# Retention stage of a hybrid diffusion step: query scaling tied to an earlier step, squares summed by ScalarE, weight halves and sums of quarters re-placed

## The chip, the core and the metric

One kernel, one core of one Trainium2 chip. The metric is the time of one execution on the device, in microseconds (us); the kernel before has a median of 1134.67 us over three runs (1134.26 to 1134.86).

## What is computed

One layer of a diffusion backbone on 640 tokens (128 of context, 512 latent; in the kernel five tiles of 128), model width 1024. Two mixers read the same normalised input: grouped-query attention and a bidirectional retention in chunks of 128 tokens. Their outputs are projected, gated, merged and projected again, and a gated MLP with a convolution follows. The change lies in the retention branch and just behind it. The reference, cut to that:

```python
def retention_scan(q, k, v, log_gamma, s0):       # chunks n of 128 tokens
    scores = einsum("bhnid,bhnjd->bhnij", qc, kc) * intra_decay
    intra  = einsum("bhnij,bhnjv->bhniv", scores, vc)
    kv     = einsum("bhnjd,bhnjv->nbhdv", kc * k_decay, vc)
    s_final, s_prev = scan(lambda s, kv_n: chunk_decay * s + kv_n, s0, kv)
    cross  = einsum("bhnid,nbhdv->bhniv", qc * q_decay, s_prev)
    return intra + cross, s_final

def retention_branch(...):                         # both directions, 8 heads, dk 64, dv 128
    o = rms_scale(o_f + o_b)                       # o * rsqrt(mean(o*o) + eps), per token and head
    return silu(rg) * o, s_f, s_b
# then: y = sigmoid(ga) * (ya @ w_att_o) + sigmoid(gr) * (yr @ w_ret_o);  y @ w_out
```

## The kernel before

**Precision.** TensorE multiplies numbers that are split in a high and a low half (`mm3`: three products for one). A weight tile is split by `w_split`: ScalarE casts the high half (L147), and VectorE subtracts it for the low half (L152). With `lo_eng` set to "dma", ScalarE instead writes the negated weights and GpSimd's queue issues a DMA that adds on top of them (L149, L150). The tiles that hold weights before the split are called raw (two in turn), the halves wh (eight in turn).

**Stages.** Normalisation and modulation; keys, values and queries; attention; the attention's output projection; the projections for the retention; the chunk states; the retention itself; a long stage of matrix products by units ("seven"), which computes the second half of the gate, the merge gates and the retention's output projection with seven products in place of eight; then the output projection and the MLP. TensorE accumulates in PSUM banks of 512 numbers per partition: five banks named mm for `mm3` and three named aux, taken in turn.

**Chunk states** (`states`, L968 to L1002). For each of two halves hh of the heads (four heads each) and each tile t: VectorE scales the keys by their decay (L977, twice, into a tile named r2k, five in turn), TensorE multiplies them with the values (L980), ScalarE copies the result out (L985, L990, L992). Then VectorE runs the recurrence in small steps (L997 and L999, 24 each per half). Sums and differences of quarters of the input, needed later by the units (`h_sums`, L928 to L965), are interleaved, and so is the first gate projection `rg0`, an `a_group` over five banks, with two halves of 512 weight rows, twelve matmuls per tile and half (L159 to L161).

**Retention** (`retention`, ten groups (t, hh), t from 0 to 4 within each hh). Four steps per group, each step of a group standing beside other steps of its neighbours:

- `ret_q` (L1009 to L1017): four small transfers on SyncE's queue bring the queries of the group into a tile qd (four in turn, L1015). No transfer for t = 0.
- `ret_a`: TensorE transposes the keys (L1023), ScalarE copies queries and keys (L1027, L1031), VectorE multiplies qd by its decay (L1029).
- `ret_b`, one step later: score products on TensorE into an aux bank (L1040), VectorE multiplies them by the decay matrix into an r2k tile (L1042), which empties the bank.
- `ret_c`, one step later: TensorE multiplies scores with values and qd with the state into an aux bank (L1049, L1051); ScalarE squares the bank into an r2k tile (L1054) and copies it over the values (L1055); VectorE reduces the squares to four sums (L1056, into sso).
- `ret_d`, after each five groups: the root of the sums of squares, twenty numbers per partition (on VectorE by three Newton steps, L210 to L222, for hh = 0; through a power on GpSimd for hh = 1), then the scaling of the outputs, one tile at each step.

`rg0` goes on in between; `evac_rg` (L1113 to L1116) applies the gate to the outputs as its banks finish.

**What sets the order.** Through these stages a scheduler places the instructions of TensorE, VectorE and ScalarE by its own estimate of when each can go; the code's order is only its input. `tc.issue_after(x)` makes what is issued inside it come after x. From L1342 on the engines keep the order in which the code is written (`manual_schedule`): `ret_unit` and `in_unit` prepare weight halves (ScalarE's cast L1173, VectorE's subtraction L1193), and a list `plan` of pairs (n, step) says behind which product n of the sequence each further step is issued. Through `plan` go the transposed outputs (`yr_block`, L1365 and L1370), and the halves of their quarters and sums of quarters: L1414 subtracts two quarters into yx, `y_hi` (L1394) casts the high half on ScalarE, `y_lo` (L1397) subtracts it on VectorE, `low_dma` (L1381) makes a low half by a ScalarE activation and an accumulating DMA, and `own_low` calls `low_dma` for a quarter itself (yr.c). L1224 finishes a column of the gate out of an aux bank.

## Time and profile before

| | |
|---|---|
| median of three runs | 1134.67 us |
| the profiled execution | 1134.39 us |
| its span, first to last instruction | 1132.6 us |
| TensorE busy | 1100.2 us, 97% of the span |
| VectorE busy | 877.2 us, 77% |
| ScalarE busy | 630.5 us, 56% |
| granted TensorE clock | 0.997 |

By stretches of the profiled execution, TensorE is busy 47.0 of 47 us from 391 to 438 us (the state products with the value projection), 18.8 of 22 from 438 to 460, 35.7 of 37 from 460 to 497 (the retention), 61.2 of 63 from 497 to 560 (the first units), and 100.0 of 100 from 560 to 660.

How to read the rows that follow: a row of a timeline has the start in us, the duration in us, the engine (PE is TensorE's matmul, DVE VectorE, ACT ScalarE, POOL GpSimd, SP SyncE), the line, the operation, the tile written and the tiles read, the shape, and how many instructions of that kind were joined; in brackets stands the time that the engine was idle ahead of it and what ended that. Matmul durations overlap, so TensorE's rate is read from start to start. A row of waits names the waiting instruction, the instruction that released it, and the idle time. A row of transfers has the tile, its source, the queue, the count, the size and the median us from issue to landing. A row of stretches has the length, and for each of TensorE's matmuls, weight loads, VectorE, ScalarE and GpSimd the busy time and the count, then clock, DMA share and GB/s; for one line alone, only the engines that it uses.

### The profile page before, as it was taken

The numbers are of one execution on the slowest core, as the hardware profiler recorded it, in microseconds if no ns is written. First come the engines' busy times: TensorE is split into PE (matmuls) and PEld (weight loads), VectorE is DVE, ScalarE is ACT, GpSimd is POOL, SyncE is SP. The second block draws the span as 40 slices with busy tenths as digits, with TensorE's granted clock in tenths as the row PEclk, the third lists the DMA queues.
The fourth block names the chain that finished last, engine by engine and source line by source line (L and its number), as shares of the span: only waits on it lengthen the run. The fifth ranks groups of instructions, "written<-read, shape, count | busy, mean of one in ns | idle before, by whom it ended". The sixth has DMA issues, their size and how long they took to land.

```text
span 1132.6 us, 17807 instructions
## 1 busy us (share of the span) xinstructions
PE 1100.2 (97%) x6757; PEld 1004.1 (89%) x6757; DVE 877.2 (77%) x1524; ACT 630.5 (56%) x1198; POOL 165.7 (15%) x189
## 2 busy tenths in 40 slices
...
GB/s 301 251 152 71 47 38 38 1 38 218 298 170 162 254 67 112 50 67 136 131 163 164 282 135 193 131 112 130 142 140 160 153 77 166 130 130 163 128 130 93
DMA packets 147350, 156.47 MB, mean 138 GB/s; under 512 B 28200, under 2 KB 117880, under 8 KB 147008
## 3 DMA queue, kind: packets, MB, share of 16 engines
...
q14 instruction: 33, 0.27, 0.1%
...
## 4 chain that ended last, share of the span: by engine, by line
PE 79%; DVE 9%; issue 4%; ACT 3%; DMA 3%; SPq 3%; POOL 0%; DVEq 0%; POOLq 0%; ACTq 0%
SPq L1015 1%; DMA weights.raw.1_114<-in_w_in 1%; DVE mod.acc.34_3970 L294 1%; SPq L325 1%; DVE mod.acc.25_3630 L294 1%; DMA weights.raw.266_7916<-in_w_down 1%; DVE x1.u1.1_6520 L1673 1%; DMA const.u1.1_70<-in_cst 0%; SPq L331 0%; DMA ret2.qd.9_4625<-ret.u4.4_3422 0%; DVE x1.u1.1_6520 L1722 0%; DVE ret2.u1.1_4272 L999 0%; DVE ret.u4.4_3422 L881 0%; DVE x1.u1.1_6520 L1480 0%; PE mm3.mm.72_6360 L1146 0%
## 5 line engine op out<-in xcount | busy, mean ns | idle before, releaser
...
L1810 DVE TENSOR_TENSOR t7.u4.4_7008<-t7.u4.4_7008,const.u1.1_70 128x320 f32<-128x320 f32 x10 | 4.9, 493 | 11.2 <-ACT const.u1.1_70 L1809 11.2
L429 ACT CAST acts.u1.1_90<-f0.s.2_104 128x640 fp32r<-128x640 f32 x4 | 2.9, 727 | 9.8 <-DVE f0.s.2_104 L427 9.8
L299 POOL DMA_DIRECT2D mod.acc.25_3630<-in_b_mod x2 | 1.7, 855 | 42.4 <-ACT ret.u4.4_3422 L874 42.4
L152 DVE TENSOR_TENSOR weights.wh.113_4462<-weights.raw.111_4459,weights.wh.112_4461 128x1024 fp32r<-128x1024 f32 x1 | 1.2, 1226 | 8.6 <-ACT weights.wh.112_4461 L147 8.6
L584 POOL TENSOR_TENSOR p1.u1.1_604<-p1.u3.3_608,p1q.u1.1_598 128x512 f32<-128x512 f32 x1 | 1.3, 1294 | 44.6 <-DMA p1.u4.4_610<-in_cache_k 44.6
L446 PE MATMUL aux1.aux.1_134<-const.u1.1_70,xin.u1.1_72 80*128 80x80 f32 x1 | 0.4, 364 | 7.3 <-DMA xin.u1.1_72<-in_b_mod 7.3
L553 ACT ACTIVATE f0.s.3_710<-f0.s.3_710,p1q.ny20.11_878 128x128 f32<-128x128 f32 x20 | 6.0, 389 | 2.5 <-DVE p1q.ny20.11_878 L220 2.5
L147 ACT CAST weights.wh.67_3284<-weights.raw.66_3282 128x1024 fp32r<-128x1024 f32 x1 | 1.1, 1052 | 11.3 <-PE mm3.mm.8_3125 L198 11.3
L147 ACT CAST weights.wh.77_3520<-weights.raw.76_3518 128x1024 fp32r<-128x1024 f32 x1 | 1.1, 1054 | 11.2 <-PE mm3.mm.16_3382 L198 11.2
L1232 ACT ACTIVATE rt.u1.1_5101<-rt.u1.1_5101 128x640 f32<-128x640 f32 x8 | 5.9, 737 | 1.5 <-DVE rt.u1.1_5101 L1160 1.5
L429 ACT CAST acts.u1.1_90<-f0.s.1_103 128x640 fp32r<-128x640 f32 x4 | 2.9, 726 | 6.9 <-DVE f0.s.1_103 L427 6.8
L1684 DVE TENSOR_TENSOR x1.u1.1_6520<-x1.u1.1_6520,gate.u1.1_6506 128x512 f32<-128x512 f32 x10 | 6.7, 685 | 0.0
L1717 POOL TENSOR_TENSOR x1.u1.1_6520<-x1.u1.1_6520,weights.raw.441_11079 128x512 f32<-128x512 f32 x3 | 4.9, 1634 | 12.2 <-ACT x1.tm.111_11092 L1690 9.4
L997 DVE SCALAR_TENSOR_TENSOR ret2.u1.1_4272<-ret2.u1.1_4272,const.u10.10_86 64x128 f32<-64x128 f32 x24 | 6.7, 337 | 0.0
L999 DVE SCALAR_TENSOR_TENSOR ret2.u1.1_4272<-ret2.u1.1_4272,const.u10.10_86 64x128 f32<-64x128 f32 x24 | 6.6, 382 | 0.1
L553 ACT ACTIVATE p1.u4.4_610<-p1.u4.4_610,p1.ny10.15_660 128x128 f32<-128x128 f32 x10 | 3.0, 389 | 6.4 <-DVE p1.ny10.15_660 L220 6.4
L446 PEld LDWEIGHTS aux1.aux.1_134<-const.u1.1_70,xin.u1.1_72 80*128 80x128 f32 x1 | 0.2, 180 | 7.2 <-issue 7.2
L269 ACT ACTIVATE mod.wm.41_4253<-aux3.aux.5_4243 128x512 f32<-128x512 f32 x1 | 0.6, 597 | 10.6 <-issue 10.6
L152 DVE TENSOR_TENSOR weights.wh.83_3656<-weights.raw.81_3653,weights.wh.82_3655 128x1024 fp32r<-128x1024 f32 x1 | 1.2, 1224 | 6.8 <-ACT weights.wh.82_3655 L147 6.8
L553 ACT ACTIVATE f0.s.4_959<-f0.s.4_959,p1q.ny20.20_1127 128x128 f32<-128x128 f32 x20 | 6.2, 399 | 0.0
L299 POOL DMA_DIRECT2D mod.acc.34_3970<-in_b_mod x2 | 1.5, 750 | 31.7 <-PE mm3.mm.31_3941 L161 31.5
...
## 6 DMA issues: line engine op xcount, KB each, us to landing
...
p0.u5.5_119<-in_w_mod SPq DMA_DIRECT2D x2, 1024.0 KB, 10.2
p0.u6.6_125<-in_w_mod SPq DMA_DIRECT2D x2, 1024.0 KB, 15.3
p0.u7.7_128<-in_w_mod SPq DMA_DIRECT2D x2, 1024.0 KB, 12.1
gate.u1.1_6506<-spill.u3.3_2892 SPq DMA_DIRECT2D x2, 1024.0 KB, 11.5
...
```

The lines of the kernel that those rows point to most:

```text
L294: V.scalar_tensor_tensor(d, ws[n], sc, d, op0=ALU.mult, op1=ALU.add)
L325: nc.sync.dma_start(w[:, v], src.rearrange("(k p) n -> p k n", p=P))
L429: nc.scalar.copy(hT[0][:, k, :], xk)
L553: nc.scalar.activation(x[:, j], x[:, j], AF.Copy, scale=rstd[:, j:j + 1])
L997: V.scalar_tensor_tensor(Ss[0:64, hh, st + 1, j], Ss[0:64, hh, st, j], cdsel[0:64, h:h + 1], Ss[0:64, hh, st + 1, j], op0=ALU.mult, op1=AL ...
L999: V.scalar_tensor_tensor(Ss[64:128, hh, 2 - st, j], Ss[64:128, hh, 3 - st, j], cdsel[64:128, h:h + 1], Ss[64:128, hh, 2 - st, j], op0=ALU. ...
L1015: nc.sync.dma_start(q4d[64 * c:64 * c + 64, :, b, :], qr[64 * b:64 * b + 64, 2 * hh:2 * hh + 2, t * P:(t + 1) * P])
L1232: nc.scalar.activation(x, x, AF.Tanh, scale=0.5)
L1673: V.tensor_add(x1[:, t, gs], x1[:, t, gs], down_mul(ps, t, c0))
L1684: V.tensor_mul(x1[:, t, gs], x1[:, t, gs], gb[:, t == 0, gs])
L1717: eng.tensor_mul(x, x, fg[:, c0:c0 + 512])
L1810: V.tensor_sub(his[1], his[1], u3[i])
```

## The change

Five edits. (1) In `ret_a` the multiplication of qd by its decay is issued behind the last entry of a new list `behind`, which collects VectorE's key scalings of `states` and its score multiplications of `ret_b` in the order in which they are written. (2) In `ret_c` the one square over 512 columns becomes four over 128 columns, each with an accumulated sum written to sso; the reduction on VectorE is gone. (3) `rg0` takes its low halves by "dma" for its second half of weight rows (in `a_group` the choice is now for the second half alone; the groups that leave it open are as before). (4) In `plan` L1414 moves from 14 to 13, `y_hi(3)` from 15 to 16, the low half of that sum goes from `low_dma` at 16 to `y_lo(3)` at 18. (5) `own_low((0, 0), "c")` goes from 13 to 20. The lines of the kernel after are two to four higher from L968 on: 977 is 979, 997 and 999 are 999 and 1001, 1029 is 1032, 1040 and 1042 are 1043 and 1045, 1049 and 1051 are 1052 and 1054.

```diff
--- before.py
+++ after.py
@@ -178,7 +178,7 @@
             if first:
                 wh, wl = first[half]()
             else:
-                wh, wl = load_w(w[half * 512:(half + 1) * 512, :], 4, 512, lo_eng)
+                wh, wl = load_w(w[half * 512:(half + 1) * 512, :], 4, 512, lo_eng if half else None)
             for t in range(NT):
                 ts = slice(t * P, (t + 1) * P)
                 for kk in range(4):
@@ -965,6 +965,8 @@
             V.tensor_sub(hs[4][1][:, k], h4[:, k], hs[4][0][:, k].bitcast(F32))
             yield
 
+    behind = []
+
     def states():
         for hh in range(2):
             hs = slice(4 * hh, 4 * hh + 4)
@@ -974,7 +976,7 @@
                 kvl = r2k().rearrange("p (h c d) -> p h c d", h=4, c=2)
                 kin = rk[:, t, :].rearrange("p (h d) -> p h d", h=8)[:, hs, :]
                 for c in range(2):
-                    V.tensor_mul(kvl[:, :, c, :], kin, kdec[:, hs, c:c + 1].to_broadcast([P, 4, 64]))
+                    behind.append(V.tensor_mul(kvl[:, :, c, :], kin, kdec[:, hs, c:c + 1].to_broadcast([P, 4, 64])))
                 ps = aux([P, 512], tag="aux")
                 for j in range(4):
                     nc.tensor.matmul(ps[:, j * P:(j + 1) * P], kvl[:, j].rearrange("p c d -> p (c d)"),
@@ -1026,7 +1028,8 @@
             bs = slice(64 * b, 64 * b + 64)
             nc.scalar.copy(qt[bs, :, b, :], qr[bs, 2 * hh:2 * hh + 2, t * P:(t + 1) * P])
         if qd is not None:
-            V.tensor_mul(qd, qd, dq[:, hs, :].rearrange("p h i -> p (h i)"))
+            with tc.issue_after(behind[-1].ins):
+                V.tensor_mul(qd, qd, dq[:, hs, :].rearrange("p h i -> p (h i)"))
         kt = rs2([P, 256], tag="rkT", bufs=2)
         nc.scalar.copy(kt, pk[:, :256])
         return qt, qd, kt
@@ -1039,7 +1042,7 @@
                 h = 2 * j + par
                 nc.tensor.matmul(psc[:, h * P:(h + 1) * P], kt[:, j * P:(j + 1) * P], qt[:, j, par, :],
                                  start=True, stop=True)
-        V.tensor_mul(at_, psc.rearrange("p (h i) -> p h i", h=4), dmat[:, 4 * hh:4 * hh + 4, :])
+        behind.append(V.tensor_mul(at_, psc.rearrange("p (h i) -> p h i", h=4), dmat[:, 4 * hh:4 * hh + 4, :]))
         return at_
 
     def ret_c(t, hh, qd, at_):
@@ -1051,9 +1054,9 @@
                 nc.tensor.matmul(po[:, js], qd[:, js], Ss[:, hh, t - 1, j, :], start=False, stop=True)
         p3 = po.rearrange("p (h v) -> p h v", h=4)
         sq = r2k().rearrange("p (h v) -> p h v", h=4)
-        nc.scalar.activation(sq, p3, AF.Square)
+        for j in range(4):
+            nc.scalar.activation(sq[:, j], p3[:, j], AF.Square, accum_out=sso[:, hh, t, j:j + 1])
         nc.scalar.copy(rvv[hh][:, :, t, :], p3)
-        V.tensor_reduce(sso[:, hh, t], sq, axis=AX.X, op=ALU.add)
 
     def ret_d(hh):
         rso = sso[:, hh].rearrange("p t h -> p (t h)")
@@ -1116,7 +1119,7 @@
             V.tensor_mul(ov, ov, th.rearrange("p (h d) -> p h d", h=4))
         return f
 
-    rg0 = a_group(w_in[:, O_RG:O_RG + 512], hTk, mm, evac_rg(0))
+    rg0 = a_group(w_in[:, O_RG:O_RG + 512], hTk, mm, evac_rg(0), "dma")
     next(rg0)
     for i, _ in enumerate(st):
         next(hsum)
@@ -1411,8 +1414,8 @@
         plan = [(0, lambda: nc.scalar.copy(hs[3][0], h3)), (1, h_lo)]
         plan += [(3 + 2 * t, lambda: next(norm2[0], None)) for t in range(NT)]
         plan += [(4 + 2 * t, lambda t=t: yr_block(0, t)) for t in range(NT)]
-        plan += [(14, lambda: V.tensor_sub(yx, yf[0, 0], yf[1, 0])), (15, lambda: y_hi(3, f0_pair())),
-                 (16, lambda: low_dma(ys[3][1], yx)), (13, lambda: own_low((0, 0), "c"))]
+        plan += [(13, lambda: V.tensor_sub(yx, yf[0, 0], yf[1, 0])), (16, lambda: y_hi(3, f0_pair())),
+                 (18, lambda: y_lo(3)), (20, lambda: own_low((0, 0), "c"))]
         for t in range(NT):
             ts = slice(t * P, (t + 1) * P)
             plan += [(n_rg + t, lambda t=t: yr_block(1, t)),
```

On VectorE, in the second part of the chunk states (u1.1 of ret2 is the state tile, raw.116 a tile that `h_sums` uses for a difference of quarters, hs.b tiles its results; qd.4 to qd.9 are queries of the first groups). Before:

```order
L939 SCALAR_TENSOR_TENSOR weights.raw.116_4490<-weights.raw.116_4490,acts.u1.1_90 128x640
L997 SCALAR_TENSOR_TENSOR ret2.u1.1_4272<-ret2.u1.1_4272,const.u10.10_86 64x128 x4
L1029 TENSOR_TENSOR ret2.qd.5_4577<-ret2.qd.5_4577,ret.u2.2_3418 128x512
L941 TENSOR_TENSOR weights.raw.116_4490<-weights.raw.116_4490,acts.u2.2_91 128x640
L939 SCALAR_TENSOR_TENSOR weights.raw.116_4490<-weights.raw.116_4490,acts.u1.1_90 128x640
L1029 TENSOR_TENSOR ret2.qd.7_4591<-ret2.qd.7_4591,ret.u2.2_3418 128x512
L997 SCALAR_TENSOR_TENSOR ret2.u1.1_4272<-ret2.u1.1_4272,const.u10.10_86 64x128 x4
L1029 TENSOR_TENSOR ret2.qd.9_4625<-ret2.qd.9_4625,ret.u2.2_3418 128x512
L941 TENSOR_TENSOR weights.raw.116_4490<-weights.raw.116_4490,acts.u2.2_91 128x640
L948 TENSOR_TENSOR hs.b.4_4267<-weights.raw.116_4490,hs.b.3_4266 128x640
L999 SCALAR_TENSOR_TENSOR ret2.u1.1_4272<-ret2.u1.1_4272,const.u10.10_86 64x128 x12
L977 TENSOR_TENSOR ret.r2k.26_4481<-ret.u3.3_3421,const.u11.11_87 128x4x64 x2
```

After:

```order
L939 SCALAR_TENSOR_TENSOR weights.raw.116_4490<-weights.raw.116_4490,acts.u1.1_90 128x640 x2
L999 SCALAR_TENSOR_TENSOR ret2.u1.1_4272<-ret2.u1.1_4272,const.u10.10_86 64x128 x4
L941 TENSOR_TENSOR weights.raw.116_4490<-weights.raw.116_4490,acts.u2.2_91 128x640 x2
L999 SCALAR_TENSOR_TENSOR ret2.u1.1_4272<-ret2.u1.1_4272,const.u10.10_86 64x128 x4
L948 TENSOR_TENSOR hs.b.4_4267<-weights.raw.116_4490,hs.b.3_4266 128x640 x2
L928 TENSOR_TENSOR hs.b.5_4268<-acts.u1.1_90 128x640
L1001 SCALAR_TENSOR_TENSOR ret2.u1.1_4272<-ret2.u1.1_4272,const.u10.10_86 64x128 x12
L979 TENSOR_TENSOR ret.r2k.26_4481<-ret.u3.3_3421,const.u11.11_87 128x4x64 x2
L979 TENSOR_TENSOR ret.r2k.27_4504<-ret.u3.3_3421,const.u11.11_87 128x4x64 x2
L979 TENSOR_TENSOR ret.r2k.28_4515<-ret.u3.3_3421,const.u11.11_87 128x4x64 x2
L979 TENSOR_TENSOR ret.r2k.29_4538<-ret.u3.3_3421,const.u11.11_87 128x4x64 x2
L1032 TENSOR_TENSOR ret2.qd.4_4572<-ret2.qd.4_4572,ret.u2.2_3418 128x512
```

The multiplications of qd.4, qd.5, qd.7 and qd.9 stood between the steps of the recurrence; now qd.4 stands behind all key scalings of the second half, the other three further on, and both pieces of L948 and one of L928 ahead of the twelve steps of L1001 (L999 before).

On TensorE, ahead of the output sums in aux.31 (which takes the bank of aux.28, the output sums of the group before; mm.41 is a bank of the gate projection). Before:

```order
L1023 MATMUL aux3.aux.29_4768<-const.u1.1_70,ret.u3.3_3421 128x128 x2
L1040 MATMUL aux3.aux.30_4776<-ret2.u2.2_4273,ret2.rkT.13_4711 128x128 x4
L159 MATMUL mm3.mm.41_4455<-weights.wh.118_4725,acts.u1.1_90 128x512
L1049 MATMUL aux3.aux.31_4783<-f0.s.5_3419,ret.r2k.35_4715 128x128
L1051 MATMUL aux3.aux.31_4783<-ret2.u1.1_4272,ret2.qd.7_4591 128x128
```

After:

```order
L1025 MATMUL aux3.aux.29_4776<-const.u1.1_70,ret.u3.3_3421 128x128 x2
L1043 MATMUL aux3.aux.30_4784<-ret2.u2.2_4273,ret2.rkT.13_4715 128x128 x4
L159 MATMUL mm3.mm.41_4455<-weights.wh.118_4729,acts.u1.1_90 128x512
L160 MATMUL mm3.mm.41_4455<-weights.wh.119_4730,acts.u1.1_90 128x512
L161 MATMUL mm3.mm.41_4455<-weights.wh.118_4729,acts.u2.2_91 128x512
L1052 MATMUL aux3.aux.31_4791<-f0.s.5_3419,ret.r2k.35_4719 128x128
L1054 MATMUL aux3.aux.31_4791<-ret2.u1.1_4272,ret2.qd.7_4591 128x128
```

Of the gate's three products per weight row one stood ahead of the output sums, and now all three do.

On VectorE, where the first half's sums of squares are complete and their root begins (r2k.41 and r2k.43 are the scores of two neighbouring groups; L210 to L212 begin the root; f0.s.5 holds the outputs). Before:

```order
L1042 TENSOR_TENSOR ret.r2k.41_4828<-aux3.aux.33_4829,ret.u1.1_3417 128x512
L1116 TENSOR_TENSOR f0.s.5_3419<-f0.s.5_3419,ret.r2k.40_4809 128x4x128
L1029 TENSOR_TENSOR ret2.qd.16_4813<-ret2.qd.16_4813,ret.u2.2_3418 128x512
L965 TENSOR_TENSOR acts.u2.2_91<-ret2.u1.1_4272,acts.u1.1_90 128x2x320
L1056 TENSOR_REDUCE const.u12.12_88<-ret.r2k.42_4845 128x4
L1042 TENSOR_TENSOR ret.r2k.43_4882<-aux3.aux.36_4883,ret.u1.1_3417 128x512
L210 TENSOR_SCALAR ret2.nm20.18_4849<-const.u12.12_88 128x20
L211 TENSOR_SCALAR ret2.ni20.19_4850<-ret2.nm20.18_4849 128x20
```

After:

```order
L1045 TENSOR_TENSOR ret.r2k.41_4838<-aux3.aux.33_4839,ret.u1.1_3417 128x512
L1119 TENSOR_TENSOR f0.s.5_3419<-f0.s.5_3419,ret.r2k.40_4819 128x4x128
L1032 TENSOR_TENSOR ret2.qd.14_4771<-ret2.qd.14_4771,ret.u2.2_3418 128x512
L210 TENSOR_SCALAR ret2.nm20.18_4861<-const.u12.12_88 128x20
L1045 TENSOR_TENSOR ret.r2k.43_4894<-aux3.aux.36_4895,ret.u1.1_3417 128x512
L211 TENSOR_SCALAR ret2.ni20.19_4862<-ret2.nm20.18_4861 128x20
L1032 TENSOR_TENSOR ret2.qd.16_4823<-ret2.qd.16_4823,ret.u2.2_3418 128x512
L212 TENSOR_SCALAR ret2.ny20.20_4863<-ret2.ni20.19_4862 128x20
```

The reduction is gone, the multiplications of qd.14 and qd.16 each stand behind a score multiplication (r2k.41, r2k.43), and the first steps of the root lie between them. On SyncE's queue the load of raw.127 (1 MB) and the four transfers of qd.16 have changed places: the load is now first. On GpSimd's queue the first of `rg0`'s two accumulating DMAs stands ahead of the stores of the second half's new states, the second behind them.

## The prediction

> **What bounds the kernel now.** I read the first part of the page, then TensorE's list of waits, then the timelines of the engine that each wait names.
>
> ```profile
> span 1132.6 us, 17807 instructions
> PE 1100.2 (97%) x6757; PEld 1004.1 (89%) x6757; DVE 877.2 (77%) x1524; ACT 630.5 (56%) x1198; POOL 165.7 (15%) x189
> ```
> ```profile
> PE aux3.aux.13_4484 L980 <- DVE ret.r2k.26_4481 L977: 2.9, 1, 2.9
> PE aux3.aux.61_5526 L1365 <- DVE rt.u1.1_5101 L1224: 1.8, 1, 1.8
> PE aux3.aux.36_4883 L1040 <- DVE ret.r2k.41_4828 L1042: 1.3, 1, 1.3
> ```
>
> In a wait's row the three figures are the sum of the idle time, how often it came, and the longest. TensorE sets the end: 97% busy, and the change leaves it the same matmuls, since it touches only where other engines' work stands. All the change can give back is its idle time inside the stages that it touches: these three waits and one of 0.3 at L1049, quoted below: 2.9 + 1.8 + 1.3 + 0.3 = 6.3 us. (Longer ones lie in stages that the change does not touch.) All it can cost is new idle time there, or a wait pushed into the stages behind. Line numbers are those of before. I then read, for each of them, the engine named as its releaser, back to the first idle time in that engine's own queue: that is where a change of order can act.
>
> **Wait 1, L980 (2.9 us).** TensorE, ScalarE and VectorE just ahead of it (start, duration, engine; in brackets the idle time ahead and its releaser):
>
> ```profile
> 434.23 1.05 PE L980 MATMUL aux3.aux.11_4397<-f0.s.5_3419,ret.r2k.23_4394 128*128 128x128 f32 x8
> 438.06 1.26 ACT L945 CAST hs.b.3_4266<-weights.raw.116_4490 128x1280 fp32r<-128x1280 f32 x1 [3.06 <-DVE weights.raw.116_4490 L941]
> 436.60 0.69 DVE L1029 TENSOR_TENSOR ret2.qd.9_4625<-ret2.qd.9_4625,ret.u2.2_3418 128x512 f32<-128x512 f32 x1 [2.68 <-DMA ret2.qd.9_4625<-ret.u4.4_3422]
> 439.43 0.83 DVE L948 TENSOR_TENSOR hs.b.4_4267<-weights.raw.116_4490,hs.b.3_4266 128x640 fp32r<-128x640 f32 x1 [1.40 <-ACT hs.b.3_4266 L945]
> 440.28 3.31 DVE L999 SCALAR_TENSOR_TENSOR ret2.u1.1_4272<-ret2.u1.1_4272,const.u10.10_86 64x128 f32<-64x128 f32 x12
> 443.61 0.76 DVE L977 TENSOR_TENSOR ret.r2k.26_4481<-ret.u3.3_3421,const.u11.11_87 128x256 f32<-128x256 f32 x2
> 444.51 1.13 PE L980 MATMUL aux3.aux.13_4484<-f0.s.6_3420,ret.r2k.26_4481 128*128 128x128 f32 x8 [2.85 <-DVE ret.r2k.26_4481 L977]
> 458.85 0.69 DVE L1042 TENSOR_TENSOR ret.r2k.30_4604<-aux3.aux.19_4605,ret.u1.1_3417 128x512 f32<-128x512 f32 x1
> 459.69 1.13 PE L1049 MATMUL aux3.aux.22_4648<-f0.s.5_3419,ret.r2k.30_4604 128*128 128x128 f32 x8 [0.35 <-ACT ret2.u3.3_4274 L1027]
> ```
>
> VectorE stood 2.68 us for a query transfer that nobody needed yet; the cast L945, the twelve state updates L999 and the key scaling L977 were queued behind it. The change puts all four query multiplications of this stretch behind the second half's L977: 2.7 us of waiting and 4 x 0.6 us of work leave the queue. What is late next: L999 reads ScalarE's copy of aux.11, whose matmuls end at 434.23 + 1.05 = 435.3. With the copy's half microsecond that is 435.9. VectorE's own queue is little later: in the new order both halves of L948 and one L928 stand ahead of L999, 3 x 0.8 us of the fourth row's size; ScalarE's cast for them no longer waits for qd.9, and by my count they end at about 436.4. Then 3.31 for L999 and half of the pair's 0.76 put both L977 at about 440.5; TensorE wants them at 444.51 - 2.85 = 441.7. Cover 1.2 us, and the idle time goes whole: **-2.9**. The 0.3 us at L1049 goes too: the profile puts it down to ScalarE, but the r2k.30 that it reads was written by L1042 up to 458.85 + 0.69 = 459.54, and that stands behind the second twelve L999 on VectorE's queue, which come earlier by what is regained: **-0.3**, at worst 0. What the moved query multiplications now stand in front of is later work on the same queue, with its 2.7 us regained; their readers, the L1051 of their groups, come a whole group later than the score product that they are tied to.
>
> **Wait 2, L1040 (1.3 us).**
>
> ```profile
> 473.11 0.69 DVE L1029 TENSOR_TENSOR ret2.qd.12_4700<-ret2.qd.12_4700,ret.u2.2_3418 128x512 f32<-128x512 f32 x1 [2.39 <-DMA ret2.qd.12_4700<-ret.u4.4_3422]
> 481.58 0.68 DVE L1042 TENSOR_TENSOR ret.r2k.41_4828<-aux3.aux.33_4829,ret.u1.1_3417 128x512 f32<-128x512 f32 x1
> 482.32 1.16 PE L1040 MATMUL aux3.aux.36_4883<-ret2.u2.2_4273,ret2.rkT.17_4824 128*128 128x128 f32 x8 [1.33 <-DVE ret.r2k.41_4828 L1042]
> ```
> The ten reductions L1056 by themselves:
> ```profile
> 455.00:510.00 55.00, 6.79 (x10) 1.00 0.49 57
> ```
>
> TensorE waits for the bank that L1042 empties. Out of VectorE's stretch go the 2.39 us for qd.12 (its multiplication now follows a score product that is later than the transfer), two reductions of 0.68 and one multiplication of 0.69: 2.4 + 2 x 0.68 + 0.69 = 4.4 us for a wait of 1.3. Against it stands only that the bank's score product itself comes no earlier than TensorE issues it; so the wait goes, and I take **-1.3** with 0.0 to 0.5 us left over for the range.
>
> **Wait 3, L1365 (1.8 us).**
>
> ```profile
> 534.93 1.27 ACT L1394 CAST f0.s.7_5457<-hs.b.5_4268 128x1280 fp32r<-128x1280 f32 x1 [1.06 <-DVE hs.b.5_4268 L1414]
> 537.15 1.25 ACT L1381 ACTIVATE f0.s.7_5457<-hs.b.5_4268 128x1280 fp32r<-128x1280 f32 x1
> 538.94 0.69 DVE L1193 TENSOR_TENSOR weights.wh.151_5479<-weights.raw.140_5253,weights.wh.151_5479 128x512 fp32r<-128x512 f32 x1 [1.85 <-ACT weights.wh.151_5479 L1173]
> 540.28 0.48 DVE L1224 SCALAR_TENSOR_TENSOR rt.u1.1_5101<-aux3.aux.58_5483,rt.u1.1_5101 128x320 f32<-128x320 f32 x1
> 540.91 0.63 PE L1365 MATMUL aux3.aux.61_5526<-const.u1.1_70,f0.s.6_3420 128*128 128x128 f32 x4 [1.84 <-DVE rt.u1.1_5101 L1224]
> ```
>
> VectorE's L1224 is late because L1193 ahead of it waits for ScalarE's cast of wh.151, and that cast stands behind the rows L1394 and L1381. Ahead of that cast the change removes L1381 (1.25) and, by moving L1414 one place earlier, the idle 1.06 of L1394: 2.3 us for 1.84. VectorE, which idled 1.85 for that cast, follows it, and L1224 with it. That leaves 0.4 us of cover, thin: any other work that the scheduler lets ScalarE take in between shows in the wait again, so I keep 0.9 us (half) as its bad end. **-1.8**. What is moved lands behind this place: the low half of the sum of quarters becomes a VectorE subtraction instead of L1381 with its accumulating DMA, estimated at 1.3 to 1.5 us by L948's kind of subtraction, and the other L1381 comes seven products later. VectorE is 77% busy over the span. Their first reader is far off:
>
> ```profile
> L1148 PE MATMUL mm3.mm.63_5969<-yr.c.4_5410,weights.wh.170_5836 x4: 309/309/309, 581.5 to 582.9; 128*128 128x320 f32 x4
> ```
>
> 40 us on, so I cost them at nothing; without that cover 1.3 to 1.5 us.
>
> **The price: squares in four pieces.** The nearest rows are ScalarE's four accumulating 128-column reads of a bank in the attention (first and last of four), beside the present single square and copy, and TensorE around them. Between two of the four stands the read of the accumulator, which the step from one to the next holds.
>
> ```profile
> 173.78 0.37 ACT L720 ACTIVATE att.P.81_1828<-aux2.aux.19_1811,att.mxc.79_1824 128x128 f32<-128x128 f32 x1
> ...
> 174.82 0.38 ACT L720 ACTIVATE att.P.81_1828<-aux2.aux.19_1811,att.mxc.79_1824 128x128 f32<-128x128 f32 x1
> ```
> ```profile
> 472.18 0.60 ACT L1054 ACTIVATE ret.r2k.37_4758<-aux3.aux.28_4749 128x512 f32<-128x512 f32 x1 [1.13 <-PE aux3.aux.28_4749 L1051]
> 472.67 0.58 ACT L1055 COPY f0.s.5_3419<-aux3.aux.28_4749 128x512 f32<-128x512 f32 x1
> ```
> ```profile
> 467.65 0.40 PE L160 MATMUL mm3.mm.40_4454<-weights.wh.119_4726,acts.u1.1_90 128*128 128x512 f32 x1
> 468.36 0.39 PE L160 MATMUL mm3.mm.40_4454<-weights.wh.119_4726,acts.u1.1_90 128*128 128x512 f32 x1
> ...
> 473.33 0.47 PE L1049 MATMUL aux3.aux.31_4783<-f0.s.5_3419,ret.r2k.35_4715 128*128 128x128 f32 x2
> ```
>
> One piece steps by (174.82 - 173.78) / 3 = 0.35, four take 4 x 0.35 = 1.4; the single square gives way to the copy after 472.67 - 472.18 = 0.49. So each bank of output sums is free 0.9 us later, ten times. ScalarE has room for ten times 0.9 (last of the rivals), and mostly TensorE comes back to the bank only after a stretch of gate matmuls. Not at aux.31, which reuses aux.28's bank: the copy ends at 473.25 and TensorE starts at 473.33, without slack. The new order puts three 512-column matmuls ahead of it where one stood, 2 x 0.24 us of cover ((468.36 - 467.65) / 3 each): 0.9 - 0.5 = **+0.4**. The order does the same at aux.40, one head group later: **+0.4**. Bounds for the two together: 0 (covered) and 2 x 0.9 = 1.8 (no cover at all). [...]
>
> The low halves of two weight tiles go from VectorE to ScalarE and an accumulating DMA:
>
> ```profile
> yr.c.4_5410<-yr.a.2_5096 POOLq DMA_DIRECT2D x1, 640.0 KB, 6.3
> weights.raw.127_5075<-in_w_in SPq DMA_DIRECT2D x1, 1024.0 KB, 5.9
> ret2.qd.14_4763<-ret.u4.4_3422 SPq DMA_DIRECT2D x4, 64.0 KB, 2.1
> ```
>
> VectorE loses two L152 of these. The nearest row, an accumulating DMA of 640 KB, lands after 6.3 us. On GpSimd's queue the first of the two stands ahead of the second half's stores of new states; these read r2k.25, whose place is needed again only for r2k.30, the 458.85 row above. ScalarE can issue these (512 KB) by about 446; the first reader is the row at 467.65. Cost 0, covered by some 15 us.
>
> **Sum.** -2.9 - 0.3 - 1.3 - 1.8 + 0.8 = -5.5. The profiled execution took 1134.39 (its span and 1.8 around it), 0.28 under the median 1134.67; 1134.39 - 5.5 = 1128.9, from the median 1129.2. I say **1129.0**.
>
> **The rivals.** *A new wait behind qd.16.* On SyncE's queue the 1 MB load raw.127 now stands ahead of qd.16's transfers, as it stood ahead of qd.22's, for which VectorE idled:
>
> ```profile
> 488.46 0.69 DVE L1029 TENSOR_TENSOR ret2.qd.22_4869<-ret2.qd.22_4869,ret.u2.2_3418 128x512 f32<-128x512 f32 x1 [1.29 <-DMA ret2.qd.22_4869<-ret.u4.4_3422]
> 491.25 0.68 DVE L1042 TENSOR_TENSOR ret.r2k.46_4927<-aux3.aux.39_4928,ret.u1.1_3417 128x512 f32<-128x512 f32 x1
> 492.94 0.27 PE L1040 MATMUL aux3.aux.42_4975<-ret2.u2.2_4273,ret2.rkT.24_4923 128*128 128x128 f32 x1
> ```
>
> qd.16 would be 5.9 - 2.1 = 3.8 us later; behind its multiplication stand the whole root chain and L1042 of r2k.46, which frees the bank of aux.42. L1042 ends 492.94 - 491.93 = 1.0 us ahead of need now, and VectorE has lost five reductions (3.4 us) and a wait before it: I see 1 to 4 us of cover, so a loss of 0 to 2.5 us and 1129 to 1131.5. [...] Chance of a loss over 1 us: 0.14. *The waits go and the squares are hidden:* 1134.4 - 6.3 = 1128.1; 0.15. *Wait 3 or 2 largely stays,* since another cast holds ScalarE: the forecast and 1.3 or 1.8, 1130.3 to 1130.8; 0.10. *Slower: ScalarE becomes the bound of the retention.* If every one of the ten groups waits for its bank, 10 x 0.9 = 9.0 against 6.3: 1137.1. It decides where the copies end after the next need of the bank at every group. Against it:
>
> ```profile
> 456.00:504.00 48.00, 46.33 (x323) 42.10 (x322) 40.78 (x83) 28.22 (x60) 3.63 (x5) 1.00 0.54 58
> ```
>
> ScalarE (fourth figure) has 28.2 of 48 us there, and 37 with the pieces. 0.04. *The order does not move:* 1134.5; 0.05, as the instruction order shows the moves and only their effect is in doubt.
>
> **How the numbers follow.** Forecast 0.52, the five rivals 0.48. The range takes in full cover (1128.1) less the spread of the runs, and the loss behind qd.16 or a wait that stays: 1127.8 to 1131.6; it leaves out the slower case, the unmoved one and tails. A measurement here tells 0.2% (2.3 us) from no change: all cases under 1132.4 are faster, 0.88; no change 0.08; slower 0.04.
>
> **What would show it.** Right: L980 of aux.13 and L1365 of aux.61 without idle time; L1054 at four pieces of 0.35 us; short idle times at aux.31 and aux.40 with ScalarE's L1055 as releaser. Wrong: idle time at aux.42 or 43 put down to L1042 (the transfer), or at most groups put down to L1055 (ScalarE), or 1.8 us still at aux.61.

## The result and the profile after

The changed kernel takes 1126.09 us (median of four runs, 1125.21 to 1126.9) against 1134.76 (1134.26 to 1135.06): ratio 0.9924, interval 0.9907 to 0.9941. With more rounds it was 1126.24 against 1134.58, 0.9925 (0.9913 to 0.9938). Forecast were 1129.0 and a range down to 1127.8: the sign and the four waits were right, but 8.3 to 8.7 us came where 5.5 were forecast.

The profiled execution took 1125.21 (before: 1134.39). The page after, first part, and TensorE's list of waits (in part):

```profile
span 1123.3 us, 17862 instructions
PE 1098.1 (98%) x6757; PEld 1003.3 (89%) x6757; DVE 871.4 (78%) x1513; ACT 636.5 (57%) x1269; POOL 165.4 (15%) x190
```
```profile
PE aux1.aux.1_134 L446 <- DMA xin.u1.1_72<-in_b_mod: 7.0, 1, 7.0
PE mm1.mm.1_161 L391 <- DVE xin.u2.2_102 L382: 5.2, 1, 5.2
PE aux1.aux.4_264 L404 <- DMA p0.u4.4_116<-in_w_mod: 0.6, 1, 0.6
...
PE aux3.aux.72_7097 L1503 <- ACT x1.row.46_6982 L1513: 0.3, 1, 0.3
```

Nothing of the four waits is left; what remains is the start-up, and waits of 0.6 and less in stages that the change does not touch. Where they were, VectorE and TensorE now look so (lines of the kernel after). Wait 1:

```profile
432.76 1.56 DVE L948 TENSOR_TENSOR hs.b.4_4267<-weights.raw.116_4490,hs.b.3_4266 128x640 fp32r<-128x640 f32 x2 [0.84 <-ACT hs.b.3_4266 L945]
435.09 3.32 DVE L1001 SCALAR_TENSOR_TENSOR ret2.u1.1_4272<-ret2.u1.1_4272,const.u10.10_86 64x128 f32<-64x128 f32 x12
438.42 0.76 DVE L979 TENSOR_TENSOR ret.r2k.26_4481<-ret.u3.3_3421,const.u11.11_87 128x256 f32<-128x256 f32 x2
440.01 1.05 PE L982 MATMUL aux3.aux.13_4484<-f0.s.6_3420,ret.r2k.26_4481 128*128 128x128 f32 x8
```

The recurrence runs straight on from L948 and L928, the key scaling ends at 439.2, 0.8 us ahead of its reader. Wait 2:

```profile
469.69 0.68 DVE L1032 TENSOR_TENSOR ret2.qd.12_4704<-ret2.qd.12_4704,ret.u2.2_3418 128x512 f32<-128x512 f32 x1
474.71 0.68 DVE L1045 TENSOR_TENSOR ret.r2k.41_4838<-aux3.aux.33_4839,ret.u1.1_3417 128x512 f32<-128x512 f32 x1
475.72 1.06 PE L1043 MATMUL aux3.aux.36_4895<-ret2.u2.2_4273,ret2.rkT.17_4834 128*128 128x128 f32 x8
```

qd.12 is there when its multiplication's turn comes, and L1045 empties the bank 0.3 us before TensorE wants it. Wait 3, on ScalarE and TensorE:

```profile
528.46 1.25 ACT L1397 CAST f0.s.7_5494<-hs.b.5_4268 128x1280 fp32r<-128x1280 f32 x1
529.61 0.62 ACT L1176 CAST weights.wh.151_5496<-weights.raw.140_5275 128x512 fp32r<-128x512 f32 x1
532.55 0.60 PE L1368 MATMUL aux3.aux.61_5544<-const.u1.1_70,f0.s.6_3420 128*128 128x128 f32 x4
```

The cast of wh.151 follows one cast instead of a cast, an idle microsecond and an activation.

### The profile page after: what moved, and what is told of

Its sections match the earlier page's. It is cut to its first block, busy times and chain, and to the rows that moved or that the text cites. A ratio compares the mean times of both kernels' runs of the same rounds, so it can differ in the third digit from the quotient of the medians.

```text
span 1123.3 us, 17862 instructions
## 1 busy us (share of the span) xinstructions
PE 1098.1 (98%) x6757; PEld 1003.3 (89%) x6757; DVE 871.4 (78%) x1513; ACT 636.5 (57%) x1269; POOL 165.4 (15%) x190
## 4 chain that ended last, share of the span: by engine, by line
PE 90%; DVE 4%; ACT 2%; DMA 2%; issue 1%; SPq 1%; ACTq 0%; DVEq 0%
DMA p0.u4.4_116<-in_w_mod 1%; DVE x1.u1.1_6541 L1676 1%; DMA weights.raw.266_7937<-in_w_down 0%; DMA xin.u1.1_72<-in_c_ctx 0%; SPq L331 0%; DVE x1.u1.1_6541 L1725 0%; PE mm3.mm.57_5730 L1149 0%; DVE x1.u1.1_6541 L1483 0%; PE mm3.mm.72_6381 L1149 0%; DVE acts.u2.2_91 L432 0%; PE mm1.mm.11_294 L161 0%; PE mm7.mm.8_7748 L1799 0%; PE mm3.mm.69_6246 L1152 0%; PE mm3.mm.66_6117 L1152 0%; PE mm7.mm.50_10241 L1798 0%
## 5 line engine op out<-in xcount | busy, mean ns | idle before, releaser
L152 DVE TENSOR_TENSOR weights.wh.113_4462<-weights.raw.111_4459,weights.wh.112_4461 128x1024 fp32r<-128x1024 f32 x1 | 1.2, 1226 | 8.6 <-ACT weights.wh.112_4461 L147 8.6
L1001 DVE SCALAR_TENSOR_TENSOR ret2.u1.1_4272<-ret2.u1.1_4272,const.u10.10_86 64x128 f32<-64x128 f32 x24 | 6.6, 381 | 1.2 <-ACT ret2.u1.1_4272 L994 1.1
L147 ACT CAST weights.wh.77_3520<-weights.raw.76_3518 128x1024 fp32r<-128x1024 f32 x1 | 1.1, 1051 | 11.2 <-PE mm3.mm.16_3382 L198 11.2
L999 DVE SCALAR_TENSOR_TENSOR ret2.u1.1_4272<-ret2.u1.1_4272,const.u10.10_86 64x128 f32<-64x128 f32 x24 | 6.7, 336 | 0.5 <-ACT ret2.u1.1_4272 L992 0.5
L152 DVE TENSOR_TENSOR weights.wh.83_3656<-weights.raw.81_3653,weights.wh.82_3655 128x1024 fp32r<-128x1024 f32 x1 | 1.2, 1226 | 6.6 <-ACT weights.wh.82_3655 L147 6.6
```

The lines of the kernel that those rows point to most:

```text
L147: nc.scalar.copy(hi, rv)
L152: (lo_eng or V).tensor_sub(lo, rv, hi.bitcast(F32))
L999: V.scalar_tensor_tensor(Ss[0:64, hh, st + 1, j], Ss[0:64, hh, st, j], cdsel[0:64, h:h + 1], Ss[0:64, hh, st + 1, j], op0=ALU.mult, op1=AL ...
L1001: V.scalar_tensor_tensor(Ss[64:128, hh, 2 - st, j], Ss[64:128, hh, 3 - st, j], cdsel[64:128, h:h + 1], Ss[64:128, hh, 2 - st, j], op0=ALU. ...
```

## The experiments

All fifteen runs carry out the whole computation; seven add work, as said there. Times are medians; "before" is the kernel before, run beside them on the same chip (1134.58 us with the first four, 1135.19 with the next four, 1133.95 with the next four, 1135.3 with the last three). The changed kernel itself ran only for the result and with the first four; before moves by up to 1.4 us between these sets, so a difference between the changed kernel's 1126.2 and a run of a later set is known no better than to about 1 us.

After the first traces two things were suspected beside the four waits: that an idle TensorE loses clock afterwards, and that the change acts on the wait ahead of acc.11, 250 us behind the last line it touches. The runs bear out both, with the limits said below.

### The changed kernel again

> The changed kernel once more, with more rounds. Theory (the four waits are worth their start-to-start loss, 3.0 + 0.5 + 1.5 + 2.0 = 7.0 us, the squares cost nothing, and what was gained beyond that lies in transfers that take longer or shorter from run to run): the four waits are gone again, idle time at the start-up and ahead of acc.11 (0.9 us in the kernel before) comes or stays away independently of the change; median 1126 to 1128. Rival (the change also frees acc.11, 250 us further on, for 1.0 us, through the times at which its loads meet other transfers): no idle time ahead of acc.11 in this run either, and median at most 1126.5.

1126.24, ratio 0.9925 (0.9913 to 0.9938). Nothing ahead of acc.11 again. New is a short wait at aux.42:

```profile
487.44 1.16 PE L1043 MATMUL aux3.aux.42_4991<-ret2.u2.2_4273,ret2.rkT.24_4937 128*128 128x128 f32 x8 [0.27 <-DVE ret.r2k.46_4941 L1045]
```

### One edit alone, or one undone

Edit 1 alone (with its list as in the change), against the kernel before:

```diff
-            V.tensor_mul(qd, qd, dq[:, hs, :].rearrange("p h i -> p (h i)"))
+            with tc.issue_after(behind[-1].ins):
+                V.tensor_mul(qd, qd, dq[:, hs, :].rearrange("p h i -> p (h i)"))
```

> Edit 1 alone: the query multiplications behind the key scalings and score products; squares, weight halves and plan as before. Theory: waits 1 and 2 and the 0.3 at L1049 go, since each came from a query multiplication that stood waiting on VectorE's queue (2.7 and 2.4 us); aux.61 keeps its 1.8. 3.0 + 0.5 + 1.5 = 5.0 us less than before, about 1129.7. Rival (wait 2 needs the reductions out of VectorE's queue too): 1.3 us stay at aux.36 and the gain is 3.5, about 1131.2.

1129.38, ratio 0.9954 (0.994 to 0.9967): 5.2 us. aux.13 and aux.36 have no wait, aux.22 keeps 0.3, aux.61 its 1.8, and acc.11 waits 1.1. Wait 2 did not need the reductions gone; the 0.3 at aux.22, which the theory had going too, did not go with edit 1.

Edits 4 and 5 alone, against the kernel before:

```diff
-        plan += [(14, lambda: V.tensor_sub(yx, yf[0, 0], yf[1, 0])), (15, lambda: y_hi(3, f0_pair())),
-                 (16, lambda: low_dma(ys[3][1], yx)), (13, lambda: own_low((0, 0), "c"))]
+        plan += [(13, lambda: V.tensor_sub(yx, yf[0, 0], yf[1, 0])), (16, lambda: y_hi(3, f0_pair())),
+                 (18, lambda: y_lo(3)), (20, lambda: own_low((0, 0), "c"))]
```

> Edits 4 and 5 alone: the five steps of the plan re-placed, all else as before. Theory: only the wait at aux.61 goes, 1.84 us idle and 0.16 of restart, 2.0 us less: about 1132.7; aux.13 and aux.36 keep 2.9 and 1.3. Rival (acc.11's wait goes with this edit): 3.0 us less, about 1131.7, with no idle time ahead of acc.11.

1133.59, ratio 0.9986 (0.9977 to 0.9995), between 0.6 and 2.6 us. The wait at aux.61 is gone, acc.11 waits 1.2. The profiled execution ran at half clock for some microseconds behind the wait at aux.13 (granted clock 0.50 from 444 to 446 us), which takes part of the gain back.

Edit 2 undone, against the changed kernel:

```diff
-        for j in range(4):
-            nc.scalar.activation(sq[:, j], p3[:, j], AF.Square, accum_out=sso[:, hh, t, j:j + 1])
+        nc.scalar.activation(sq, p3, AF.Square)
         nc.scalar.copy(rvv[hh][:, :, t, :], p3)
+        V.tensor_reduce(sso[:, hh, t], sq, axis=AX.X, op=ALU.add)
```

> The changed kernel with edit 2 undone: one square of 512 columns and the reduction on VectorE again; edits 1, 3, 4 and 5 stay. Theory: the four pieces cost and bring nothing at TensorE; all four waits stay away and the time is that of the changed kernel within 0.5 us (1126 to 1128). Rival (without the ten reductions of 0.68 us gone, VectorE is late again at aux.36): 1.3 to 1.5 us of idle time there, about 1128 to 1129. What the prediction had (pieces cost 0.8): 0.8 us faster than the changed kernel.

1126.13, ratio 0.9926 (0.9913 to 0.9938): the changed kernel's time, as the theory had it, but not for its reason. In the profile the four waits stay away, the retention is 0.3 to 0.8 us quicker than in the seven profiles that have edits 1 and 2, and acc.11 waits 1.1: two terms of opposite sign, whose sum is too small to show in the medians.

Edits 4 and 5 undone, the diff of edits 4 and 5 above the other way round:

> The changed kernel with edits 4 and 5 undone (the plan as before). The wait at aux.61 comes back, 1.84 us idle and 0.16 of restart: 2.0 us over the changed kernel's 1126.2. Theory now (a TensorE that stood still for some 2 us or more can fall to half clock for some us afterwards: granted clock 0.50 in 538 to 540 us of the run with edit 1 alone, none in the profile of before): in part of the executions 1.5 to 2 us more, so a median of 1128.2 to 1129.5, a spread over 1.5 us, and granted clocks below 0.998 in some. Rival (the wait costs its idle time and nothing else): 1128.2, spread and clock of the changed kernel (0.998 in every run).

1128.99, ratio 0.9942 (0.993 to 0.9954), from 1127.47 to 1130.24: 2.8 over the changed kernel for a wait of 1.9, with granted clocks of 0.998, 0.997 and three times 0.996. The theory's side.

Edit 2 alone, the diff of the one-square run the other way round on the kernel before:

> Edit 2 alone on the kernel before: four squares with accumulated sums, no reduction. Theory: the waits at aux.13 and aux.61 stay (2.9 and 1.8), that at aux.36 shrinks since two reductions of 0.68 leave VectorE's queue ahead of it; 1133 to 1134.5; and the wait ahead of acc.11 is the load raw.266's own, so it does not go by this edit for sure. Rival (the wait ahead of acc.11 goes by this edit, as it stayed away in both runs that have it and came in the four that don't): no idle time ahead of acc.11, raw.266 lands in 5.0 us instead of 6.2 to 6.5, and 1 us less in the time by that.

1135.64, ratio 1.0005 (0.9995 to 1.0015): no gain by itself. acc.11 does not wait and raw.266 takes 5.3 us: here the rival was right, and my theory wrong. The microsecond does not show in the median. One reason is the price of the pieces, which this order does not cover:

```profile
478.50 0.49 PE L1049 MATMUL aux3.aux.34_4844<-f0.s.5_3419,ret.r2k.38_4781 128*128 128x128 f32 x2 [0.59 <-ACT f0.s.5_3419 L1056]
```

TensorE waits for ScalarE's copy behind the four squares, and from the first matmul of aux.28 to that of aux.42 it takes 23.8 us where before took 22.7. Waits of 2.6 and 1.8 stay as well, and seven of the twelve runs have a granted clock of 0.995.

Edit 3 undone, against the changed kernel:

```diff
-    rg0 = a_group(w_in[:, O_RG:O_RG + 512], hTk, mm, evac_rg(0), "dma")
+    rg0 = a_group(w_in[:, O_RG:O_RG + 512], hTk, mm, evac_rg(0))
```

> The changed kernel with edit 3 undone: the low halves of the second half of rg0 on VectorE (two subtractions of 1.22 us). Theory: VectorE has the room; the time of the changed kernel within 0.5 us (1126 to 1126.7), no wait at the state products. Rival: the two subtractions stand ahead of the recurrence steps and TensorE waits 1 to 2.4 us at a state or score product of the second half: 1127.2 to 1128.6.

1126.54, ratio 0.9923 (0.991 to 0.9936). In the medians the low halves by DMA are worth nothing that shows. In the profile the wait at aux.22 is back:

```profile
455.39 1.16 PE L1052 MATMUL aux3.aux.22_4648<-f0.s.5_3419,ret.r2k.30_4604 128*128 128x128 f32 x8 [0.29 <-DVE ret.r2k.30_4604 L1045]
```

VectorE's two L152 stand ahead of the second half's recurrence, 1.1 us each, and L1045 behind it ends too late. From the first matmul of aux.13 to that of aux.22 it takes 15.0 us here and with edit 1 alone, and 14.6 in the changed kernel: it is edit 3 that removes this wait.

Edit 1 undone, against the changed kernel:

```diff
-            with tc.issue_after(behind[-1].ins):
-                V.tensor_mul(qd, qd, dq[:, hs, :].rearrange("p h i -> p (h i)"))
+            V.tensor_mul(qd, qd, dq[:, hs, :].rearrange("p h i -> p (h i)"))
```

> The changed kernel with edit 1 undone: the query multiplications stand where the scheduler puts them. Waits 1 and the 0.3 at L1049 come back (3.5 us start to start), wait 2 perhaps (1.5). Theory (an idle stretch of 2 us or more can be followed by half clock): 3.5 to 5.0 us and a further 0.5 to 1.7 on the median over the changed kernel's 1126.2, 1130 to 1132.5, with granted clocks below 0.998 in most runs. Rival (idle time and restart only): 1129.7 to 1131.2 with 0.998 in every run.

1130.99, ratio 0.9965 (0.9953 to 0.9977): 4.8 over the changed kernel. aux.13 waits 2.3, aux.36 0.9, and aux.34 0.5 for ScalarE's copy behind the squares. The time lies in the range of both theories, and three of five runs show 0.998: this run does not decide between them, though its profile has half clock behind the wait at aux.13 (0.56 from 442 to 444 us).

### What a wait costs: the clock

One or four more casts of 1.25 us ahead of wh.151's, the same values written again (the diff of one; five in place of two for four):

```diff
-            nc.scalar.copy(ys[m][0], yx)
+            for _ in range(2 if m == 3 else 1):
+                nc.scalar.copy(ys[m][0], yx)
```

> The changed kernel with ScalarE's cast of the high half of the third sum of quarters done twice (1.25 us more ahead of the cast of wh.151, which holds up aux.61). The cover there is about 0.4, so TensorE should wait about 0.8 at aux.61. Theory (idle stretches of some 2 us are followed by 3.4 us or so at half clock, short ones are not): 1.0 us over the changed kernel's 1126.2, granted clock 0.997 to 0.998 in every run as there. Rival (any wait can bring the clock down): 1 to 2.7 us over, clock 0.996 in some.

1127.2, ratio 0.994 (0.9926 to 0.9954): 1.0 over, for 0.8 of wait, and granted clocks of 0.997 and 0.998, as the theory had it.

> The same with the cast done five times, 5.0 us more: TensorE should wait about 4.5 us at aux.61. Theory (half clock after it, in every execution): 4.5 + 0.2 + 1.7 to 2 = 6.4 to 6.7 us over the changed kernel's 1126.2, about 1132.7, granted clock 0.996 in every run, 0.5 in the 3 to 4 us behind the wait. Rival (idle time alone): 4.7 over, 1130.9, clock as the changed kernel's.

1133.26, ratio 0.9991 (0.9982 to 0.9999): 7.1 over, for 4.7 of wait; every run's clock is 0.995 or 0.996. That is well over the rival's 4.7 and 0.4 above the theory's range. Stretches of both, the first figure behind the engines being the granted clock. One cast more:

```profile
530.00:534.00 4.00, 3.35 (x24) 3.09 (x23) 1.76 (x4) 3.97 (x8) 0.77 (x1) 1.00 0.94 187
534.00:538.00 4.00, 3.83 (x28) 3.85 (x29) 4.00 (x8) 2.39 (x6) 1.27 (x1) 1.00 0.49 56
```

Four casts more:

```profile
534.00:538.00 4.00, 0.00 (x0) 0.00 (x0) 1.44 (x3) 3.97 (x8) 0.00 (x0) 1.00 0.00 0
538.00:542.00 4.00, 3.51 (x16) 3.54 (x17) 4.00 (x7) 1.73 (x4) 1.27 (x1) 0.57 0.40 44
542.00:546.00 4.00, 4.00 (x32) 3.98 (x31) 3.36 (x6) 2.92 (x5) 0.00 (x0) 1.00 0.20 21
```

After 0.8 us of standing still the clock stays whole; after 4.7 it is 0.57 over the next 4 us, in which 16 matmuls start instead of some 30. In the profiles here half clock followed six of ten waits of 1.8 to 2.9 us as well; what decides among those ten is not shown. Ahead of the last 10 us of the programs the profiles hold eight stretches at half clock, and each adds up to 1.7 us of lost clock, which is 3.4 us at half.

### Moving an instruction fetch

```diff
         nc.tensor.transpose(ps[:, :80], crow, ident[:80, :80])
+        for _ in range(8):
+            nc.tensor.transpose(ps[:, 128:208], crow, ident[:80, :80])
```

> The changed kernel with eight more transposes of the same constant at its start, into columns that nobody reads, while TensorE waits for the first tokens anyway: 16 more instructions (a weight load and a matmul each) in TensorE's stream. So far, in the four kernels with one square, a fetch of a block of instructions falls 2.75 to 3.5 us after the issue of the 1 MB load raw.266, the load takes 6.2 to 6.5 us and TensorE waits 0.9 to 1.2 ahead of acc.11; in the six with four squares it falls at 4.25 to 4.5, the load takes 5.0 to 5.3 and nobody waits. The four-square kernels have 7 waiting instructions fewer in TensorE's stream up to there. Theory (the fetch delays the load, and the change moved the fetch): 16 instructions more bring the block fetch about 1.2 us earlier (256 instructions a block, one every 20 us), to about +3.1; the load takes 6.2 or more, acc.11 waits about 1.0, and the time is 1.0 over the changed kernel's 1126.2. Rival (the squares act in another way, or the loads differ by chance): 5.0 us and no wait, 1126.2.

1126.85, ratio 0.9937 (0.9924 to 0.995). The fetch came earlier than I had worked out, 0.7 us behind the load's issue (the 256 instructions a block are an estimate; the page of before has 53 packets of instructions on queue q8 in 1132.6 us, one every 21 us, and 13514 matmuls and weight loads, which is 255 to a packet if all of q8 is TensorE's); raw.266 took 5.5 us, and acc.11 waited 0.2. Between the two theories, so inconclusive by itself; the transposes also lengthen the start, by some 1.7 us in the profile.

Thirty of them, with edit 2 undone as well:

```diff
+        for _ in range(30):
+            nc.tensor.transpose(ps[:, 128:208], crow, ident[:80, :80])
```

> The changed kernel with one square and the reduction again (as in an earlier run, where acc.11 waited 1.1) and thirty more transposes at the start, 60 instructions in TensorE's stream, while TensorE is idle there for 5 us. Theory: the block fetch comes 4.7 us earlier, ahead of raw.266's issue; the load takes 5.0 to 5.3 us and the wait ahead of acc.11 goes, without the four squares: 1.0 us under that run in the profile, unless the start is longer by the transposes. Rival (the squares themselves do it): 6.2 us and 1.1 of wait as in that run, 1126.1.

1129.11, ratio 0.9962 (0.9948 to 0.9975). With one square and no fetch near the load, acc.11 does not wait; the start is 4.0 us longer, which hides the gain in the time. Issued behind VectorE's copy of the bank, the same thirty lie in TensorE's idle time:

```diff
         V.tensor_copy(cv.rearrange("p i k -> p (i k)"), ps[:, :80])
+        for _ in range(30):
+            nc.tensor.transpose(ps[:, 128:208], crow, ident[:80, :80])
```

> The changed kernel with one square and the reduction again, and thirty transposes at the start as in an earlier run, but issued behind VectorE's copy of the first bank, so that they lie in TensorE's idle 5 us there and hold up nothing. Theory: raw.266 lands in 5.0 us, no wait ahead of acc.11 (1.1 to 1.3 less than with one square alone), and the retention is without the price of the four pieces (0.3 to 0.4 less than the changed kernel): 1125.2 to 1125.8, under the changed kernel's 1126.2. Rival (the wait ahead of acc.11 came in the profiled execution of the one-square kernel only, as its median of 1126.1 equals the changed kernel's): 1126.1, no gain.

1125.63, ratio 0.9914 (0.9901 to 0.9928), the lowest of all; against the changed kernel (0.9925 in its own comparison) the intervals overlap. No wait ahead of acc.11, and one of 0.9 elsewhere (mm.62, for an accumulating DMA) in the profiled execution, which no other profile has.

The same insertion in the kernel before:

> The kernel before with the same thirty transposes hidden at the start, nothing else. Theory: all four waits stay, the one ahead of acc.11 (1.1) goes: 1133.2 to 1133.9 against 1134.3 to 1134.7 of the kernel before, so some 1.0 us of the change's 8.4 is the place of an instruction fetch. Rival (the fetch matters in few executions): within 0.3 us of the kernel before.

1133.68 against 1135.3, ratio 0.9986 (0.9977 to 0.9995): 0.6 to 2.6 us from the kernel before, by thirty transposes that compute nothing. What they move is seen in the transfers of the first 4 us behind raw.266's issue (queue, packets, MB, share; then the load with its time to landing). One square:

```profile
q1 hardware_dynamic: 405, 0.83, 60.7%
q8 instruction: 1, 0.02, 1.4%
...
weights.raw.266_7917<-in_w_down SPq DMA_DIRECT2D x1, 1024.0 KB, 6.4
```

One square, thirty transposes hidden:

```profile
q1 hardware_dynamic: 420, 0.86, 64.9%
...
weights.raw.266_7947<-in_w_down SPq DMA_DIRECT2D x1, 1024.0 KB, 5.1
```

The changed kernel:

```profile
q1 hardware_dynamic: 431, 0.88, 61.5%
...
weights.raw.266_7937<-in_w_down SPq DMA_DIRECT2D x1, 1024.0 KB, 5.0
```

With a packet of instructions (q8) among the load's, the load lands 1.3 us later; without it in these 4 us, it takes 5.0 to 5.1. In the changed kernel the packet falls 4.4 us behind the issue, when the load is nearly through. All seventeen profiles agree: a packet 2.8 to 3.8 us behind the issue goes with 6.2 to 6.5 us (four profiles), one at 4.4 to 4.7 with 5.0 to 5.3 (nine), one 2.6 to 2.9 us ahead of it with 5.0 to 5.1 (three), and one 0.7 behind it with 5.5. The packet's 1.4% of the 4 us of 16 engines is 0.9 us of one engine; that the load's part on that engine comes later by this is an estimate, not shown.

The same kernel showed in its profiled execution, the slowest of its eleven at 1134.71, what the waits can cost in an execution of before:

```profile
440.00:444.00 4.00, 1.37 (x7) 0.98 (x6) 3.99 (x15) 0.79 (x2) 1.23 (x2) 0.85 0.33 66
444.00:448.00 4.00, 4.00 (x17) 3.46 (x17) 4.00 (x10) 1.53 (x2) 0.00 (x0) 0.73 0.00 0
...
542.00:545.00 3.00, 3.00 (x14) 2.96 (x13) 1.62 (x4) 1.56 (x4) 0.42 (x1) 0.50 1.16 175
```

Half clock behind the wait at aux.13 (2.6 us) and again behind that at aux.61 (1.8 us).

### More of the price

The four squares done twice each:

```diff
-        for j in range(4):
-            nc.scalar.activation(sq[:, j], p3[:, j], AF.Square, accum_out=sso[:, hh, t, j:j + 1])
+        for j in range(8):
+            nc.scalar.activation(sq[:, j % 4], p3[:, j % 4], AF.Square, accum_out=sso[:, hh, t, j % 4:j % 4 + 1])
```

> The changed kernel with each of the four squares done twice: eight pieces at 0.255 us, the bank of output sums free another 1.0 us later. Theory (the two gate products more that the order puts ahead of aux.31 and aux.40 just cover four pieces; 0.1 and 0.25 us over the one-square kernel there): without cover left, 1.0 us each at aux.31 and aux.40, and a share at the other groups: 2 to 4 us over the changed kernel, 1128.2 to 1130.2. Rival (there is a microsecond of cover left, the squares are free): 1126.2 to 1126.8. If ScalarE were near its bound in the retention, ten groups at 1.0: 1136.

1134.65, ratio 0.9992 (0.9983 to 1.0001): 8.4 us over the changed kernel, more than either theory gave. The largest wait is not for a bank that ScalarE holds:

```profile
PE aux3.aux.40_4974 L1052 <- DVE ret.r2k.46_4965 L1045: 3.7, 1, 3.7
```
```profile
482.33 0.69 DVE L1032 TENSOR_TENSOR ret2.qd.16_4839<-ret2.qd.16_4839,ret.u2.2_3418 128x512 f32<-128x512 f32 x1 [3.31 <-DMA ret2.qd.16_4839<-ret.u4.4_3422]
```

The output sums in aux.40 read r2k.43, which was written long before, and ScalarE had emptied the bank of aux.37 at 483.97; yet they start at 486.88, just as VectorE ends r2k.46. Why this order has them wait for that row is not shown. r2k.46 stands behind the root behind qd.16 on VectorE, the path of the prediction's first rival. A wait of 1.2 us ahead of mm.45 and half clock behind the wait at aux.40 (0.50 from 488 to 490 us) come on top. So this run mixes the price with a new order and does not measure the pieces' cover alone.

## Why the prediction was wrong

**The four waits: mechanism right, size short.** By starts in the two profiled executions, TensorE between the last matmul before and the first after the wait:

```profile
441.27 0.39 PE L161 MATMUL mm3.mm.40_4454<-weights.wh.114_4465,acts.u2.2_91 128*128 128x512 f32 x1
```
```profile
439.78 0.39 PE L161 MATMUL mm3.mm.40_4454<-weights.wh.114_4465,acts.u2.2_91 128*128 128x512 f32 x1
```

Before, aux.13 started at 444.51, 3.24 us after the first row; after, at 440.01, 0.23 after the second. The wait was worth 3.0, not 2.85. In the same way 0.5, 1.5 and 2.0 for the others, 7.0 in all where I had 6.3. "All the change can give back is its idle time" was the step that failed first: the idle time is counted to the modelled end of a matmul, and each wait costs 0.16 more, since matmuls that follow each other overlap (in the rows above one lasts 0.39 us, and the next starts 0.23 behind it). The term of 0.3 came true by luck: the prediction had the wait at aux.22 go by what edit 1 regains on VectorE, but with edit 1 alone it stayed, and it came back without edit 3, which the prediction had at nothing.

**The pieces: the row I took was the wrong one.**

```profile
466.99 0.28 ACT L1058 ACTIVATE ret.r2k.37_4764<-aux3.aux.28_4755 128x128 f32<-128x128 f32 x1 [1.13 <-PE aux3.aux.28_4755 L1054]
467.16 0.19 ACT L1058 ACTIVATION_READ_ACCUMULATOR ret.r2k.37_4764<-aux3.aux.28_4755 128x1 f32 x1
467.25 0.27 ACT L1058 ACTIVATE ret.r2k.37_4764<-aux3.aux.28_4755 128x128 f32<-128x128 f32 x1
...
468.00 0.60 ACT L1059 COPY f0.s.5_3419<-aux3.aux.28_4755 128x512 f32<-128x512 f32 x1
```
```profile
468.65 0.49 PE L1052 MATMUL aux3.aux.31_4791<-f0.s.5_3419,ret.r2k.35_4719 128*128 128x128 f32 x2
```

A piece with its accumulator read steps by 0.25, four by 468.00 - 466.99 = 1.01, not 1.4; the attention's 0.35 belonged to another kind of activation. So the bank comes 0.5 us later (1.01 less the 0.49 after which the single square gave way to the copy), and the two more gate products hide nearly all: the copy ends at 468.60 and TensorE starts at 468.65. Against the kernel with one square, from the first matmul of aux.36 to that of aux.42 (first that kernel, then the changed one):

```profile
475.96 1.06 PE L1043 MATMUL aux3.aux.36_4885<-ret2.u2.2_4273,ret2.rkT.17_4826 128*128 128x128 f32 x8
486.47 1.06 PE L1043 MATMUL aux3.aux.42_4977<-ret2.u2.2_4273,ret2.rkT.24_4925 128*128 128x128 f32 x8
```
```profile
486.50 1.16 PE L1043 MATMUL aux3.aux.42_4991<-ret2.u2.2_4273,ret2.rkT.24_4937 128*128 128x128 f32 x8
```

10.51 with one square, 486.50 - 475.72 = 10.78 with four: 0.3, and 0.1 more from the first matmul of aux.28 to that of aux.34, for the 0.8 forecast. But this profile is of the quickest of the four executions. In the seven profiles that have edits 1 and 2 (without the doubled squares) the two stretches cost 0.3 to 0.8 together, the most of it for a reason that the term did not have and that follows.

**The rival behind qd.16 happened, almost under cover, and by edit 2.** SyncE's queue (start, and how long the issuing took) with one square, then in the changed kernel:

```profile
470.72 5.55 SPq L1017 DMA_DIRECT2D ret2.qd.16_4815<-ret.u4.4_3422  x4
476.37 0.53 SPq L136 DMA_DIRECT2D weights.raw.127_5077<-in_w_in  x1
```
```profile
471.14 2.56 SPq L136 DMA_DIRECT2D weights.raw.127_5097<-in_w_in  x1
473.82 3.46 SPq L1017 DMA_DIRECT2D ret2.qd.16_4823<-ret.u4.4_3422  x4
```

With one square the load stands behind qd.16's transfers as before, VectorE does not wait for qd.16, and L1045 of r2k.46 ends 3.2 us ahead of aux.42. In the changed kernel:

```profile
481.01 0.69 DVE L1032 TENSOR_TENSOR ret2.qd.16_4823<-ret2.qd.16_4823,ret.u2.2_3418 128x512 f32<-128x512 f32 x1 [3.16 <-DMA ret2.qd.16_4823<-ret.u4.4_3422]
485.76 0.68 DVE L1045 TENSOR_TENSOR ret.r2k.46_4941<-aux3.aux.39_4942,ret.u1.1_3417 128x512 f32<-128x512 f32 x1
```

VectorE stands 3.16 us for the transfer behind raw.127, and L1045 ends at 486.44, 0.06 before aux.42 starts. In the repeat VectorE's wait was 3.57 and TensorE idled 0.27. The cover was not 1 to 4 us but none to spare.

**What the sum did not have.** First, acc.11. Before, TensorE waited there, and ScalarE's cast of raw.266 was where it began; after, the cast stood 1.1 us less for the load (last row) and TensorE did not wait:

```profile
PE acc7.acc.11_8162 L159 <- ACT gt.gt0.11_8090 L1595: 0.9, 1, 0.9
```
```profile
785.37 1.05 ACT L147 CAST weights.wh.271_8054<-weights.raw.266_7916 128x1024 fp32r<-128x1024 f32 x1 [1.50 <-DMA weights.raw.266_7916<-in_w_down]
```
```profile
776.06 1.05 ACT L147 CAST weights.wh.271_8075<-weights.raw.266_7937 128x1024 fp32r<-128x1024 f32 x1 [0.36 <-DMA weights.raw.266_7937<-in_w_down]
```

By starts it was worth 1.1 us. It came in every profile with one square and no transposes (before and three runs), and in none of the nine with four squares and no transposes; with one square it went when transposes moved the fetch. That the place of the fetch goes with the wait is shown by those runs; that the four squares move it by the waits that they save is argued: with one square, the first matmul of each output sum waits for two semaphores, with four for one, and TensorE's stream has 26 instead of 33 separate wait instructions from 430 to 500 us. So in the profiles edit 2 gains 1.1 us far behind and loses 0.3 to 0.8 in place, by nothing that it was written for. The prediction named a wait pushed into the stages behind only as a cost, and put a gain there at nothing without a reason.

Second, the clock. A wait of about 2 us can be followed by half clock, which cost 1.4 us more by starts where it fell behind aux.61 (42.1 us instead of 40.7 from its first matmul to that of mm.63) and 1.0 to 1.3 behind aux.13. Before's profiled execution had none, so its page could not show it; its 15 runs beside the first experiments span 1133.24 to 1136.56, the changed kernel's five 1125.45 to 1126.4, and 11 of the 15 have a granted clock of 0.996 or less where the five have 0.998. The waits, the price in place and acc.11 make 7.3 to 7.8 of the 8.3 to 8.7 (7.0 - 0.8 + 1.1 to 7.0 - 0.3 + 1.1); the rest, 0.5 to 1.4, fits the lost clock, but its share in the medians was not measured by itself.

The two profiled executions also differ by 1.3 us at the start, where the kernels are alike (the first matmul of the attention's output projection stands at 260.70 and 259.37 us): that is taken as chance, and is part of why they stand 9.2 apart. The range failed with the sum: its lower end took full cover of the squares and no gain beyond the idle time.
